# Hybrid SSD / RG-LRU layer on one core: the masked products of four chunks built and issued as one group

## The chip, the core and the metric

The program runs on one NeuronCore of a Trainium2 chip. The metric is the device time of one execution in microseconds (us); the kernel before was timed three times, with a median of 2409.85 us (2408.59 to 2413.37). One further execution was profiled; it took 2411.09 us.

## What is computed

One layer of a diffusion backbone over 1024 latent tokens of width 1024, with 256 context tokens as a prefix. A Mamba-2 SSD branch and an RG-LRU branch, both in two directions, are gated, merged and projected; a squared-ReLU MLP follows. Only the SSD branch matters here. Its core for one direction, cut down:

```
# 8 chunks of 128 tokens, 8 groups, 4 heads a group, head width 64, state 128
cum   = cumsum(dt * a_neg) within a chunk
seg   = cum[i] - cum[j];  decay = exp(where(i >= j, seg, -inf))
cb    = C @ B^T                                   # 128 x 128 per chunk and group
y     = (cb * decay) @ (x * dt)                   # the masked product, within a chunk
      + (C @ h_start) * exp(cum)                  # what the state before the chunk adds
h_start[k+1] = exp(cum_end) * h_start[k] + B^T @ (to_end * x * dt)
y_all = y_forward + flip(y_backward) + d * x
```

All arithmetic is fp32. Large products are made of three fp32r products of high and low parts; the small products of the SSD branch are plain fp32.

## The kernel before

The kernel is written tile by tile; a scheduler then puts the instructions of each engine in a fixed order by a priority (the place in the program text, moved by `tc.high_priority(offset=...)`) and by its own estimate of when operands are ready, and adds the semaphores. Each engine runs its own order strictly. Buffers come from pools: `bufs=n` says how many copies of a tile exist, and a copy is written again only when all readers of the last tile in it are done.

The part around the change is the SSD stage. It loops over 8 groups (`g`). For a group the projections of B, C and two 128-channel tiles of x are made (`proj`, `mm3`, lines 113 to 115, PSUM tiles `acc`), convolved and put through SiLU (lines 228 to 236, 441, 442). `cb` holds C times B for all 8 chunks. For each of the two tiles (`tl`, two heads each):

- the x tile is transposed to token order, `xt` (one buffer, named xtm in the trace);
- the states `H` of all chunk borders are built in both directions (line 519 on TensorE, 527 on VectorE; one buffer);
- two halves (`hf_`) of four chunks each follow. A half has three PSUM tiles `y[0]`, `y[1]`, `y[2]` (3 buffers for all). For each chunk `p`: ScalarE makes four 128x128 exponentials `L` (line 549) from `R`, which a DMA filled and GpSimd masked (line 544); VectorE adds the two directions into `M` (line 552) and multiplies by `cb` (553); TensorE forms the forward and the backward state product (555, 556) and, for each of the two heads, the masked product (558). The head's product has 64 output rows, so the two heads' products go to the two halves of `y[2]`'s partitions and use 64 columns of the array each;
- after the four chunks VectorE takes the three `y` tiles out of PSUM: lines 560 (twice), 562, 563, 564, 565; `u` goes to DRAM by a DMA and is squared on ScalarE (569).

Projections of the next tiles (`z_tile` and the next group's B, C, x) are issued by TensorE in between, as the scheduler finds place. A row sum `rp` (462) is put in when a group's squares are ready. Every fp32 matmul of the SSD stage is two records in the trace (two passes); an `acc` matmul is one.

Of the kernel before, what the change touches and what calls it, by code (L numbers as in the profile page):

```python
# [9 lines left out]
F32 = mybir.dt.float32  # L10
F32R = mybir.dt.float32r
AF = mybir.ActivationFunctionType
OP = mybir.AluOpType
# [42 lines left out]
def _ap(t, off, dims):  # L56
    return bass.AP(tensor=t.tensor, offset=t.offset + off, ap=dims)
# [3 lines left out]
def tile_hybrid_layer(ctx: ExitStack, tc: tile.TileContext, x, xc, wmod, win, wdt, lruw, wbs, wbl,  # L61
                      wout, w1, w2, vecs, rows, out, dbg=None, stop=None):
    nc = tc.nc
    V, A, P, G, Q = nc.vector, nc.scalar, nc.tensor, nc.gpsimd, nc.sync
# [53 lines left out]
    start = ctx.enter_context(ExitStack())  # L118
# [21 lines left out]
    for k in range(10):  # L140
        if k < KT:
            wm = sp_.tile([128, 2, 1024], F32, name="wm", bufs=4)
            Q.dma_start(wm, _ap(wmod, k * 128 * 1024, [[1024, 128], [8 * 128 * 1024, 2], [1, 1024]]))
            for j in range(4):
                P.matmul(mps[j], sc[:, k, :], wm[:, j // 2, (j % 2) * 512:(j % 2 + 1) * 512],
                         start=k == 0, stop=k == KT - 1)
# [320 lines left out]
    def z_tile(t):  # L467
        zts[t] = gp.tile([128, S], F32, name="z", bufs=2)

        def zcb(s, o, n, pt, zt=zts[t]):  # L470
            A.activation(zt[:, o:o + n], pt, AF.Tanh, scale=0.5)
            V.scalar_tensor_tensor(zt[:, o:o + n], zt[:, o:o + n], 1.0, pt, op0=OP.add, op1=OP.mult)
        proj(win[T_Z + t], (0, 1), zcb)


    dw2 = {m: dr.tile([128, 1024], F32, name=f"dw{m}") for m in (*range(4), *range(24, 28))}
    z_tile(0)
    for g in range(8):
        m_ = sorted(dw2)[g]
        Q.dma_start(dw2[m_], w2[m_])  # L480
        bf = gp.tile([128, TT], F32, name="bf", bufs=1)
        proj(win[T_B + g], (0, 1, 2), conv_silu(16 + g, bf))
        bt = gp.tile([128, 10, 128], F32, name="bt", bufs=1)
        to_token(bf, bt)
        xf = {}
        cf = gp.tile([128, S], F32, name="cf")
        proj(win[T_C + g], (0, 1), conv_silu(24 + g, cf))
        xf[0] = gp.tile([128, TT], F32, name="xf", bufs=3)
        proj(win[T_X + 2 * g], (0, 1, 2), conv_silu(2 * g, xf[0]))
        cb = gp.tile([128, 8, 128], F32, name="cb", bufs=1)  # L490
        for c0 in (0, 4):
            tp = misc((128, 4, 128))
            for c in range(c0, c0 + 4):
                P.matmul(tp[:, c - c0], bf[:, c * 128:(c + 1) * 128], cf[:, c * 128:(c + 1) * 128], start=True, stop=True)
            A.activation(cb[:, c0:c0 + 4], tp, AF.Copy)
        xf[1] = gp.tile([128, TT], F32, name="xf", bufs=3)
        proj(win[T_X + 2 * g + 1], (0, 1, 2), conv_silu(2 * g + 1, xf[1]))
        sqs = {}
        for tl in range(2):
            t = 2 * g + tl  # L500
            if tl == 1:
                z_tile(t)
            xt = gp.tile([128, 10, 128], F32, name="xtm", bufs=1)
            to_token(xf[tl], xt)

            H = gp.tile([128, 9, 2, 128], F32, name="H", bufs=1)
            for k0 in range(0, 9, 2):
                n = min(2, 9 - k0)
                xs = gp.tile([128, 2, 2, 128], F32, name="xs", bufs=2)
                for d_, KD in ((0, KF), (1, KB)):  # L510
                    c0 = min(KD[k0:k0 + n])
                    V.tensor_tensor(xs[:, d_, :n].rearrange("p c (h q) -> p c h q", h=2),  # L512
                                    xt[:, c0:c0 + n].rearrange("p c (h q) -> p c h q", h=2),
                                    wst[:, c0:c0 + n, d_ * 32 + 2 * t:d_ * 32 + 2 * t + 2, None].to_broadcast([128, n, 2, 64]),
                                    op=OP.mult)
                sp = misc((128, n, 2, 128))
                for k in range(k0, k0 + n):
                    for d_, KD in ((0, KF), (1, KB)):
                        P.matmul(sp[:, k - k0, d_], bt[:, KD[k]], xs[:, d_, KD[k] - min(KD[k0:k0 + n])], start=True, stop=True)  # L519
                for k in range(k0, k0 + n):  # L520
                    if k == 0:
                        A.activation(H[:, 0], sp[:, 0], AF.Copy)
                        continue
                    for d_ in range(2):
                        for h in range(2):
                            hs_2 = slice(h * 64, h * 64 + 64)
                            V.scalar_tensor_tensor(H[:, k, d_, hs_2], H[:, k - 1, d_, hs_2], dec[:, k, d_ * 32 + 2 * t + h:d_ * 32 + 2 * t + h + 1],  # L527
                                                   sp[:, k - k0, d_, hs_2], op0=OP.mult, op1=OP.add)
            for hf_ in range(2):
                y = [ps.tile([128, 512], F32, tag="y", bufs=3, name="y") for _ in range(3)]  # L530
                E = gp.tile([128, 2, 512], F32, name="E", bufs=1)
                for h in range(2):
                    Q.dma_start(E[h * 64:h * 64 + 64],
                                _ap(decum, t * 4096 + h * 1024 + hf_ * 512, [[0, 64], [2048, 2], [1, 512]]))
                for p in range(4):
                    c = hf_ * 4 + p
                    if p % 2 == 0:
                        R = gp.tile([128, 4, 256], F32, name="R", bufs=2)
                        Q.dma_start(R, _ap(dcum, t * 4096 + c * 128, [[0, 128], [1024, 4], [1, 256]]))

                        for d_ in range(2):
                            rv = R[:, 2 * d_:2 * d_ + 2, :].rearrange("p q (c i) -> p q c i", c=2)
                            sg = 1 if d_ == 0 else -1
                            G.affine_select(out=rv, in_=rv, compare_op=OP.is_ge, fill=-BIG, base=0,  # L544
                                            pattern=[[0, 2], [0, 2], [sg, 128]], channel_multiplier=-sg)
                    L = gp.tile([128, 4, 128], F32, name="L", bufs=2)
                    for q in range(4):
                        col = hf_ * 64 + (q // 2) * 32 + 2 * t + q % 2
                        A.activation(L[:, q], R[:, q, (p % 2) * 128:(p % 2 + 1) * 128], AF.Exp,  # L549
                                     bias=ncumT[:, p, col:col + 1])  # L550
                    M = gp.tile([128, 2, 128], F32, name="M", bufs=2)
                    V.tensor_tensor(M, L[:, 0:2], L[:, 2:4], op=OP.add)
                    V.tensor_tensor(M, M, cb[:, c, None, :].to_broadcast([128, 2, 128]), op=OP.mult)
                    sl = slice(p * 128, p * 128 + 128)
                    P.matmul(y[0][:, sl], H[:, 1 + c, 0], cf[:, c * 128:(c + 1) * 128], start=True, stop=True)
                    P.matmul(y[1][:, sl], H[:, 8 - c, 1], cf[:, c * 128:(c + 1) * 128], start=True, stop=True)  # L556
                    for h in range(2):
                        P.matmul(y[2][h * 64:h * 64 + 64, sl], xt[:, c, h * 64:h * 64 + 64], M[:, h], start=True, stop=True)  # L558
                for d_ in range(2):
                    V.tensor_tensor(E[:, d_], E[:, d_], y[d_], op=OP.mult)  # L560
                u = gp.tile([128, 512], F32, name="u", bufs=2)
                V.scalar_tensor_tensor(u, xf[tl][:, hf_ * 512:hf_ * 512 + 512], vec("dsk", t), y[2], op0=OP.mult, op1=OP.add)
                V.tensor_tensor(E[:, 0], E[:, 0], E[:, 1], op=OP.add)
                V.tensor_tensor(u, u, E[:, 0], op=OP.add)
                V.scalar_tensor_tensor(u, u, 0.5, zts[t][:, hf_ * 512:hf_ * 512 + 512], op0=OP.mult, op1=OP.mult)
                Q.dma_start(du[t][:, hf_ * 512:hf_ * 512 + 512], u)
                flush()
                sq = gp.tile([128, 512], F32, name="sq", tag=f"sq{tl}", bufs=2 - tl)
                A.activation(sq, u, AF.Square)
                sqs[tl, hf_] = sq  # L570
                if tl == 1:
                    V.tensor_tensor(sq, sq, sqs[0, hf_], op=OP.add)
                    pend.append((g, hf_, sq))
        if g < 7:
            z_tile(2 * g + 2)
            flush()
        else:
            for m in range(8, 16):
                merge_tile(m)
                flush()  # L580
        r8 = gp.tile([128, 8], F32, name="r8")
        Q.dma_start(r8, _ap(dss, g * 1024, [[8, 128], [1, 8]]))
        rsqrt_small(r8, r8, RMS_EPS, 8, scale=1.0 / 256.0)
        Q.dma_start(_ap(drs[g], 0, [[8, 128], [1, 8]]), r8)
# [399 lines left out]
    for th in range(2):  # L984
        tok = []
        for i in range(4):
            ti = th * 4 + i
            if ti < len(x0):
                xt = x0[ti]
# [275 lines left out]
```

## Time and profile before

| | |
|---|---|
| median of 3 runs | 2409.85 us |
| profiled execution | 2411.09 us, of it 2409.3 us span |
| TensorE busy, share of the span | 98 %, 11485 matmul records |
| VectorE, ScalarE, GpSimd busy | 76 %, 45 %, 10 % |
| granted TensorE clock, mean over the span | 0.991 |
| SSD stage | about 515 to 1324 us of the span |

TensorE has two rows in the profile: PE is the matmul, PEld the loading of the stationary operand, which lies beside earlier matmuls. A matmul's end is modelled, so "busy" says little about how densely TensorE works; the distance from one start to the next does.

### The profile page before, as it was taken

The page shows a single profiled execution, that of the slowest core. Times are in us where ns is not written, and L with a number is a line of the kernel's source. Part 1 is how long each engine was busy: PE and PEld are TensorE (multiplying, and loading weights), DVE is VectorE, ACT ScalarE, POOL GpSimd, SP SyncE. Part 2 cuts the span into 40 slices and gives each one's busy share as a digit, 9 for nine tenths or more (in the row PEclk, how much of TensorE's full clock was granted, in tenths as well). Part 3 has the DMA queues.
Part 4 walks back from the last instruction along what each step waited for, and adds up shares of the span by engine and source line. Part 5 has one row for each costly group of instructions (what it writes and reads, how often), then busy time and mean ns, then how long its engine had stood idle before and what let it go on. Part 6 is the DMA issues. An engine that isn't in the chain of part 4 may idle for free.

```text
span 2409.3 us, 31481 instructions
## 1 busy us (share of the span) xinstructions
PE 2351.3 (98%) x11485; PEld 1881.1 (78%) x11485; DVE 1841.8 (76%) x3240; ACT 1094.0 (45%) x1909; POOL 243.5 (10%) x253
## 2 busy tenths in 40 slices
PE   7998999999999999999999999999999999999998
PEld 3877888787888878787877887877778888788876
DVE  6986688778888887878888379676687554749998
ACT  2766765635343443444344354132266444435521
POOL 1000000001110110201010000000114332000004
PEclk9998999999999999999999999999999999999999
DMA  9422154323333342434333552277345333624132
GB/s 354 130 65 64 53 166 149 106 66 118 88 97 88 97 128 64 134 81 113 88 97 118 175 196 88 80 228 233 123 151 167 106 105 105 240 79 155 55 114 87
DMA packets 135235, 298.39 MB, mean 124 GB/s; under 512 B 14996, under 2 KB 47892, under 8 KB 134952
## 3 DMA queue, kind: packets, MB, share of 16 engines
q1 hardware_dynamic: 135080, 296.39, 38.7%
q8 instruction: 90, 1.47, 0.2%
q14 instruction: 65, 0.53, 0.1%
HBM read 245.40 MB, written 55.13 MB: 125 GB/s over the span
## 4 chain that ended last, share of the span: by engine, by line
PE 77%; DVE 11%; DMA 6%; ACT 3%; issue 2%; POOL 0%; SPq 0%; POOLq 0%; DVEq 0%; ACTq 0%
PE acc L114 11%; PE acc L115 11%; PE acc L113 11%; PE pd L115 4%; PE pd L113 4%; PE pd L114 4%; PE wp L114 3%; PE wp L115 3%; PE wp L113 3%; PE mo L114 3%; PE mo L115 3%; PE mo L113 3%; PE misc L519 2%; PE y L558 2%; PE y L556 1%
## 5 line engine op out<-in xcount | busy, mean ns | idle before, releaser
L114 PE MATMUL acc<-hl,wh 128*128 128x512 f32 (+1 forms) x1560 | 596.4, 382 | 0.6 <-DVE hl L182 0.6
L115 PE MATMUL acc<-hh,wl 128*128 128x512 f32 (+1 forms) x1560 | 594.2, 381 | 0.0
L113 PE MATMUL acc<-hh,wh 128*128 128x512 f32 (+1 forms) x1560 | 591.5, 379 | 2.6 <-ACT hh L177 2.6
L114 PEld LDWEIGHTS acc<-hl,wh 128*128 128x128 f32 x1560 | 295.5, 189 | 58.1 <-issue 12.9
L113 PEld LDWEIGHTS acc<-hh,wh 128*128 128x128 f32 x1560 | 295.4, 189 | 52.2 <-issue 3.1
L115 PEld LDWEIGHTS acc<-hh,wl 128*128 128x128 f32 x1560 | 295.4, 189 | 47.9 <-issue 4.5
L549 ACT ACTIVATE L<-R,cumT 128x128 f32<-128x128 f32 x512 | 163.5, 390 | 123.9 <-issue 58.1
L102 ACT ACTIVATE wh<-wr 128x1024 fp32r<-128x1024 f32 x113 | 119.5, 1057 | 212.5 <-PE acc L114 158.1
L544 POOL TENSOR_SCALAR_AFFINE_SELECT R<-R 128x512 f32<-128x512 f32 x128 | 95.1, 766 | 1112.2 <-DMA R<-dcum 687.3
L103 DVE TENSOR_TENSOR wl<-wr,wh 128x1024 fp32r<-128x1024 f32 x113 | 138.0, 1222 | 29.2 <-ACT wh L102 27.0
L114 PE MATMUL wp<-orl,olh 128*128 128x512 f32 x392 | 153.1, 391 | 2.1 <-DVE orl L611 2.1
L115 PE MATMUL wp<-orh,oll 128*128 128x512 f32 x392 | 152.6, 389 | 0.0
L113 PE MATMUL wp<-orh,olh 128*128 128x512 f32 x392 | 149.9, 390 | 0.3 <-DVE ba L659 0.3
L527 DVE SCALAR_TENSOR_TENSOR H<-H,dec,misc 128x64 f32<-128x64 f32 x512 | 104.9, 273 | 25.0 <-PE misc L519 24.1
L97 POOL TENSOR_TENSOR mv<-mv,mhalf 128x1 f32<-128x1 f32 x34 | 29.7, 874 | 789.2 <-DVE mv L96 778.7
L234 DVE SCALAR_TENSOR_TENSOR xf<-acc,cw,xf 128x504 f32<-128x504 f32 (+1 forms) x96 | 62.4, 650 | 37.3 <-ACT xf L228 35.6
L610 ACT ACTIVATE olh<-k 128x512 fp32r<-128x512 f32 x81 | 51.1, 631 | 86.1 <-PE wp L114 81.2
L114 PEld LDWEIGHTS wp<-orl,olh 128*128 128x128 f32 x392 | 73.6, 188 | 18.8 <-DVE orl L611 3.8
L113 PEld LDWEIGHTS wp<-orh,olh 128*128 128x128 f32 x392 | 74.0, 189 | 16.3 <-DVE ba L659 0.7
L950 DVE TENSOR_TENSOR xl<-wr,xh 128x512 fp32r<-128x512 f32 x75 | 67.3, 900 | 24.3 <-ACT xh L949 24.1
L115 PEld LDWEIGHTS wp<-orh,oll 128*128 128x128 f32 x392 | 73.6, 188 | 15.2
L519 PEld LDWEIGHTS misc<-xs,bt 128*128 128x128 f32 x576 | 77.1, 191 | 9.8 <-DVE xs L512 3.0
(347 smaller groups left out, 5027.5 us busy)
## 6 DMA issues: line engine op xcount, KB each, us to landing
wr<-in_win_dram SPq DMA_DIRECT2D x80, 512.0 KB, 3.7
R<-dcum SPq DMA_DIRECT2D x64, 512.0 KB, 5.2
wr<-in_w_dram SPq DMA_DIRECT2D x37, 512.0 KB, 4.2
wm<-in_wmod_dram SPq DMA_DIRECT2D x32, 512.0 KB, 3.6
E<-decum SPq DMA_DIRECT2D x64, 256.0 KB, 4.5
da<-r SPq DMA_DIRECT2D x64, 256.0 KB, 3.1
k<-da SPq DMA_DIRECT2D x26, 512.0 KB, 3.6
k<-in_w_dram SPq DMA_DIRECT2D x20, 512.0 KB, 4.2
```

What stands on the lines that cost most here:

```text
L102: A.activation(hi, src, AF.Copy)
L103: V.tensor_tensor(lo, src, hi.bitcast(F32), op=OP.subtract)
L113: P.matmul(pt, wh, mh, start=first, stop=False)
L114: P.matmul(pt, wh, ml, start=False, stop=False)
L115: P.matmul(pt, wl, mh, start=False, stop=last)
L234: V.scalar_tensor_tensor(dv[:, :, sh:], pv[:, :, :L - sh], w[k], dv[:, :, sh:], op0=OP.mult, op1=OP.add)
L519: P.matmul(sp[:, k - k0, d_], bt[:, KD[k]], xs[:, d_, KD[k] - min(KD[k0:k0 + n])], start=True, stop=True)
L527: V.scalar_tensor_tensor(H[:, k, d_, hs_2], H[:, k - 1, d_, hs_2], dec[:, k, d_ * 32 + 2 * t + h:d_ * 32 + 2 * t + h + 1], sp[:, k - k0, d ...
L544: G.affine_select(out=rv, in_=rv, compare_op=OP.is_ge, fill=-BIG, base=0, pattern=[[0, 2], [0, 2], [sg, 128]], channel_multiplier=-sg)
L549: A.activation(L[:, q], R[:, q, (p % 2) * 128:(p % 2 + 1) * 128], AF.Exp, bias=ncumT[:, p, col:col + 1])
L610: A.activation(hi, src, AF.Copy)
L950: V.tensor_tensor(ts[i][1], v, ts[i][0].bitcast(F32), op=OP.subtract)
```

## The change

A half's masks are made in one tile `M` of four chunks with one buffer (before: a tile for each chunk, two buffers). `L` holds two chunks in one buffer (before: one chunk, two buffers). VectorE adds the directions of two chunks in one instruction of 512 columns, twice in a half, and multiplies all four chunks by `cb` in one of 1024 columns. All y products of the half stand together after that: four forward state products, four backward ones, then the eight masked ones, and all of them at a priority 120 places later (`YLATE`). `u` has one buffer in place of two. The pool's size stays as it was: `M` grows by 2 KB a partition, `u` shrinks by 2 KB.

```diff
+    YLATE = -120
@@ the loop over halves
+                M = gp.tile([128, 4, 2, 128], F32, name="M", bufs=1)
                 for p in range(4):
...
-                    L = gp.tile([128, 4, 128], F32, name="L", bufs=2)
+                        L = gp.tile([128, 2, 4, 128], F32, name="L", bufs=1)
                     for q in range(4):
                         col = hf_ * 64 + (q // 2) * 32 + 2 * t + q % 2
-                        A.activation(L[:, q], R[:, q, (p % 2) * 128:(p % 2 + 1) * 128], AF.Exp,
+                        A.activation(L[:, p % 2, q], R[:, q, (p % 2) * 128:(p % 2 + 1) * 128], AF.Exp,
                                      bias=ncumT[:, p, col:col + 1])
-                    M = gp.tile([128, 2, 128], F32, name="M", bufs=2)
-                    V.tensor_tensor(M, L[:, 0:2], L[:, 2:4], op=OP.add)
-                    V.tensor_tensor(M, M, cb[:, c, None, :].to_broadcast([128, 2, 128]), op=OP.mult)
-                    sl = slice(p * 128, p * 128 + 128)
-                    P.matmul(y[0][:, sl], H[:, 1 + c, 0], cf[:, c * 128:(c + 1) * 128], start=True, stop=True)
-                    P.matmul(y[1][:, sl], H[:, 8 - c, 1], cf[:, c * 128:(c + 1) * 128], start=True, stop=True)
-                    for h in range(2):
-                        P.matmul(y[2][h * 64:h * 64 + 64, sl], xt[:, c, h * 64:h * 64 + 64], M[:, h], start=True, stop=True)
+                    if p % 2:
+                        V.tensor_tensor(M[:, p - 1:p + 1], L[:, :, 0:2], L[:, :, 2:4], op=OP.add)
+                V.tensor_tensor(M, M, cb[:, hf_ * 4:hf_ * 4 + 4, None, :].to_broadcast([128, 4, 2, 128]), op=OP.mult)
+
+                with tc.high_priority(offset=YLATE):
+                    for d_ in range(2):
+                        for p in range(4):
+                            c = hf_ * 4 + p
+                            P.matmul(y[d_][:, p * 128:p * 128 + 128], H[:, 8 - c if d_ else 1 + c, d_], cf[:, c * 128:(c + 1) * 128],
+                                     start=True, stop=True)
+                    for p in range(4):
+                        for h in range(2):
+                            P.matmul(y[2][h * 64:h * 64 + 64, p * 128:p * 128 + 128],
+                                     xt[:, hf_ * 4 + p, h * 64:h * 64 + 64], M[:, p, h], start=True, stop=True)
...
-                u = gp.tile([128, 512], F32, name="u", bufs=2)
+                u = gp.tile([128, 512], F32, name="u", bufs=1)
```

The order on TensorE before, in the second half of a group's second tile in the middle of the stage (`y<-M` is a masked product, `y<-cf,H` a state product, `acc` a projection, `rp` the row sum):

```order
3542 L113 MATMUL acc<-hh_280,wh 128x512
3543 L558 MATMUL y<-M,xtm 64x128 x2
3544 L114 MATMUL acc<-hl_281,wh 128x512
3545 L115 MATMUL acc<-hh_280,wl 128x512
3546 L462 MATMUL rp<-sq,ones 1x512
3547 L558 MATMUL y<-M,xtm 64x128 x2
3548 L113 MATMUL acc<-hh_282,wh 128x512
3549 L114 MATMUL acc<-hl_283,wh 128x512
3550 L558 MATMUL y<-M,xtm 64x128 x2
3551 L115 MATMUL acc<-hh_282,wl 128x512
```

The order on TensorE of the changed kernel, at the first half of such a tile; its lines are numbered up to eight higher, 565 is the masked and 561 the state product:

```order
3038 L114 MATMUL acc<-hl_279,wh 128x512
3039 L561 MATMUL y<-cf,H 128x128 x4
3040 L565 MATMUL y<-M,xtm 64x128 x8
3041 L561 MATMUL y<-cf,H 128x128 x8
3042 L115 MATMUL acc<-hh_278,wl 128x512
```

Masked products stood in 126 runs over the kernel, 124 of two and 2 of four matmuls; they now stand in 32 runs of eight. The state products' runs went from 151 to 72. The number of matmuls is the same.

The order on VectorE before, between the end of a first half and the second half's masks, in a group's first tile:

```order
768 L563 TENSOR_TENSOR E<-E 128x512
769 L562 SCALAR_TENSOR_TENSOR u<-xf,vt,y 128x512
770 L552 TENSOR_TENSOR M<-L 128x256
771 L564 TENSOR_TENSOR u<-u,E 128x512
772 L553 TENSOR_TENSOR M<-M,cb 128x256
773 L565 SCALAR_TENSOR_TENSOR u<-u,z 128x512
774 L552 TENSOR_TENSOR M<-L 128x256 x2
775 L553 TENSOR_TENSOR M<-M,cb 128x256 x2
```

The same place on VectorE in the changed kernel (554 is the addition, 555 the product with `cb`):

```order
724 L568 TENSOR_TENSOR E<-E,y 128x512
725 L571 TENSOR_TENSOR E<-E 128x512
726 L570 SCALAR_TENSOR_TENSOR u<-xf,vt,y 128x512
727 L554 TENSOR_TENSOR M<-L 128x512
728 L572 TENSOR_TENSOR u<-u,E 128x512
729 L573 SCALAR_TENSOR_TENSOR u<-u,z 128x512
730 L554 TENSOR_TENSOR M<-L 128x512
731 L555 TENSOR_TENSOR M<-M,cb 128x1024
```

The masks of the second half are now two additions and one product, all behind the first half's `u`, which reads `y[2]`. ScalarE has five exponentials, a square, and three exponentials between the two additions. On TensorE eight state products and 23 projections stand between the two halves' masked groups there. After the SSD stage, from the last merge tiles on, all engines' orders are the same as before.

## Rows read from the trace of the kernel before

**Rows 1.** The page, part 1: busy us, share of the span, instructions.

```profile
PE 2351.3 (98%) x11485; PEld 1881.1 (78%) x11485; DVE 1841.8 (76%) x3240; ACT 1094.0 (45%) x1909; POOL 243.5 (10%) x253
```

**Rows 2.** Busy times of the SSD stage; PEclk is the granted clock's share.

```profile
core 0: us, PE busy (x) PEld busy (x) DVE busy (x) ACT busy (x) POOL busy (x), PEclk, DMA share, GB/s
515.00:1324.00 809.00, 806.60 (x4617) 643.42 (x4616) 671.93 (x1576) 349.22 (x804) 101.18 (x127) 1.00 0.36 101
```

**Rows 3.** All waits of TensorE's matmuls in it: us in total, times, longest.

```profile
PE y L555 <- DVE H L527: 0.9, 2, 0.5
```

**Rows 4.** Timeline of TensorE matmuls near the stage's end: start, length, line, tiles, count.

```profile
1319.18 0.39 PE L114 MATMUL acc<-hl,wh 128*128 128x512 f32 x1
1319.50 0.44 PE L558 MATMUL y<-M,xtm 128*64 128x128 f32 x4
1319.87 0.50 PE L115 MATMUL acc<-hh,wl 128*128 128x512 f32 x1
1320.21 0.39 PE L113 MATMUL acc<-hh,wh 128*128 128x512 f32 x1
1320.44 0.39 PE L114 MATMUL acc<-hl,wh 128*128 128x512 f32 x1
...
1323.21 0.66 PE L558 MATMUL y<-M,xtm 128*64 128x128 f32 x8
1323.80 0.50 PE L113 MATMUL acc<-hh,wh 128*128 128x512 f32 x1
```

**Rows 5.** The same view where masked products stand between state products.

```profile
993.28 0.49 PE L556 MATMUL y<-cf,H 128*128 128x128 f32 x2
993.70 0.44 PE L558 MATMUL y<-M,xtm 128*64 128x128 f32 x4
994.07 0.71 PE L556 MATMUL y<-cf,H 128*128 128x128 f32 x4
994.62 0.83 PE L555 MATMUL y<-cf,H 128*128 128x128 f32 x6
```

**Rows 6.** Timeline of the weight loads at Rows 4's places; idle before, releaser.

```profile
1319.50 0.20 PEld L558 LDWEIGHTS y<-M,xtm 128*64 128x64 f32 x4 [0.36 <-issue]
1319.87 0.19 PEld L115 LDWEIGHTS acc<-hh,wl 128*128 128x128 f32 x1 [0.17 <-issue]
...
1323.21 0.42 PEld L558 LDWEIGHTS y<-M,xtm 128*64 128x64 f32 x8 [0.86 <-DVE M L553]
```

**Rows 7.** Waits of weight loads in the stage: us in total, times, longest.

```profile
PEld y L558 <- issue: 13.1, 39, 0.4
PEld y L558 <- DVE M L553: 3.8, 9, 0.9
```

**Rows 8.** VectorE's groups of the stage by form: busy us, mean ns, idle before.

```profile
L103 DVE TENSOR_TENSOR wl<-wr,wh 128x1024 fp32r<-128x1024 f32 x45 | 54.8, 1217 | 3.2 <-ACT wh L102 3.2
L553 DVE TENSOR_TENSOR M<-M,cb 128x256 f32<-128x256 f32 x126 | 54.2, 437 | 0.6
L552 DVE TENSOR_TENSOR M<-L 128x256 f32<-128x256 f32 x126 | 54.2, 434 | 33.8 <-PE y L558 22.2 <-ACT L L549 8.7 <-issue 1.8
L560 DVE TENSOR_TENSOR E<-E,y 128x512 f32<-128x512 f32 x62 | 41.0, 681 | 3.1 <-PE y L556 1.6 <-DMA E<-decum 1.5
L562 DVE SCALAR_TENSOR_TENSOR u<-xf,vt,y 128x512 f32<-128x512 f32 x32 | 23.9, 745 | 12.2 <-PE y L558 12.2
L564 DVE TENSOR_TENSOR u<-u,E 128x512 f32<-128x512 f32 x31 | 21.6, 696 | 0.0
```

**Rows 9.** Timeline of ScalarE: a square and a chunk's four exponentials.

```profile
1000.23 0.63 ACT L569 ACTIVATE sq<-u 128x512 f32<-128x512 f32 x1 [0.21 <-DVE u L565]
1000.77 1.26 ACT L549 ACTIVATE L<-R,cumT 128x128 f32<-128x128 f32 x4
```

**Rows 10.** Timeline, all engines: an addition and the exponentials that reuse its `L`.

```profile
998.24 0.42 DVE L552 TENSOR_TENSOR M<-L 128x256 f32<-128x256 f32 x1
...
998.74 1.28 ACT L549 ACTIVATE L<-R,cumT 128x128 f32<-128x128 f32 x4 [2.21 <-issue]
```

## The prediction

> **What bounds the kernel now.** I read the page's first part, then the windows, the waits of TensorE, and the timelines around the masked products. The page shows TensorE busy for 98 % of the span and nobody else above 76 % [rows 1]. In the SSD stage it is 806.60 of 809.00 us at a granted clock of 1.00, that is 2.4 GHz, with VectorE at 83 % and ScalarE at 43 % [rows 2], and its matmuls waited for another engine for 0.9 us in all [rows 3]. So the stage lasts as long as TensorE's list of instructions lasts, and a change in it is worth what it takes out of that list. The list is not dense, and the busy share hides it: the reader is to look at starts. A projection starts 0.23 us after the one before (1320.21 to 1320.44). With four records of masked products in between, the way from one projection's start (1319.18) to the start of the second one behind the block (1320.21) is 1.03 us, 0.57 more than two steps of 0.23 [rows 4]. Four records themselves occupy 0.37 of it (1319.50 to 1319.87); the rest is a late start ahead of the block (0.32 for 0.23) and a slow first projection behind it (0.34 for 0.23). Between state products it is the same: a record there takes 0.11; the two ahead of the block at 993.70 need 0.42 and the four behind it 0.55, so each first record behind a block is 0.11 late and the last one ahead 0.09, and 0.37 + 0.11 + 0.09 is again 0.57 [rows 5]. The weight loads tell why: the engine loads no weights for 0.36 us ahead of each block and 0.17 behind it, with "issue" as the reason [rows 6]; 39 of the blocks' gaps of that kind sum to 13.1 us [rows 7].
>
> One block at the stage's end holds eight records, since two chunks' products met there. From its start to the next projection are 0.59 us, 0.22 more than with four [rows 4], and its weights load for 0.42 against 0.20 [rows 6]. So four further records in a running block cost 0.22, and a block of their own costs 0.57: each block that is merged into another is worth 0.35 us.
>
> The Trainium skill ("TensorEngine Tiling (Array Packing)", Tiling Modes) says that changing the tiling mode, not just the tile, drains TensorE. The two gaps agree: they stand only where 128x64 weights follow 128x128 ones or the reverse. The page gives no price, so the sum goes by the rows.
>
> **The change part by part.**
>
> *Masked products in groups.* In the two orders 124 blocks of four records and 2 of eight become 32 of sixteen. Before: 124 x 0.57 + 2 x 0.79 = 72.3 us. After, a block of sixteen: 0.57 + 3 x 0.22 = 1.23, times 32 = 39.4. TensorE's list shortens by 32.9 us. No block of sixteen stands in the trace; the bounds for a further four records are 0.22 (the block of eight, whose weights load without a pause) and 0.37 (all of a block of four from its start to the next instruction). By the upper one the group costs 0.57 + 3 x 0.37 = 1.68, and the gain falls to 18.5. Below 0.22 nothing is to be expected, since 0.42 for eight loads is already twice 0.20. I take 0.22, the nearer row.
>
> *State products in groups.* Same records at 0.11; their runs fall from 151 to 72. They use the array as the projections do and no gap like that of the masked ones stands ahead of them, so I price this at nothing; the bounds are zero and one record's 0.11 for each of 79 runs, a gain of up to 8.7.
>
> *VectorE.* Per half, before: four additions of 0.434 and four products of 0.437 are 3.48 us. After: two additions of 512 columns at 0.70 (as line 564) and one product of 1024 at 1.22 (as line 103) are 2.62 [rows 8]. That is 0.86 a half and 28 us over 32 halves, on an engine that is idle for 137 us of the stage. It lies beside TensorE and is worth nothing by itself.
>
> *The new wait.* Before, a chunk's product needs its own mask alone. After, the sixteen records wait for all four masks, and with one `M`, nothing may be written into it until the last half's group is done. In the first half of a tile this costs nothing: its masks can be made during the projections of the tile and stand on VectorE ahead of the states. The second half's have to fit between the two groups. Worked out in a group's first tile, from the first half's first masked record: VectorE takes the product and the sum on `E` (0.68 and about 0.7), which waited for the state products only, and is at `u` after about 1.5 us; `u` 0.75; addition 0.70; five exponentials at 1.26/4 = 0.32, the square 0.63 that stands among them, three more: 3.2 [rows 9], since the one `L` is free only when the first addition has read it (the handover took 998.74 - 998.66 = 0.08 in before) [rows 10]; addition 0.70; product 1.22. Together 1.5 + 0.75 + 0.70 + 0.1 + 3.2 + 0.70 + 1.22 = 8.2, and 0.2 for the handover to TensorE, 8.4 us. TensorE has in the meantime: the rest of the first group, 1.0; sixteen state records at 0.11 and the slow first one, 1.9; 23 projections at 0.23 with a slow first and the late start, 5.5: 8.4 us. It is a draw. In a group's second tile, three more projections and a row sum stand there, and on VectorE two steps of the convolution and a weight split more; I take it as a draw too. Queued behind the waiting masked product on TensorE are all projections, and so everything. A draw means that some of the 16 second halves are late by a few tenths: I take 0.2 us each, 3.2 us. The bounds are 0 and, if the cover counted for nothing, 16 x 8.4 = 134 us; the nearest row is that of masks in before, where 9 gaps of weight loads that ended with a mask sum to 3.8 us, 0.36 of each being the switch, so 0.6 us of real lateness in all [rows 7]. That row lies near zero, so I stay near zero.
>
> The Trainium skill ("Perfetto Trace Analysis", Optimizing Scalar/DVE Operations) speaks against this part: where VectorE and ScalarE aren't saturated but cause bubbles on other engines, breaking instructions up may let work complete sooner. The change does the reverse, on engines at 83 and 43 %. In the trace of before they cause almost none (the 0.6 us above), so the rule would bite only if the draw is lost; its time is that of the second rival below.
>
> *Other buffers.* One `u`: its DMA and its square have until the next half's `u`, over 6 us later by the same chain; nothing. The lower priority moves no weight load and no DMA on SP's queue past another that TensorE waits for within the stage; behind the stage the orders are the same.
>
> **The sum.** 2411.1 (the profiled execution) - 32.9 + 3.2 = 2381.4 us. The profiled execution is 1.2 above the median of the runs, so 2380.
>
> **The rivals.**
>
> 1. *The wait eats everything and more (slower).* The chain of the second half's masks takes longer than its cover by over 32.9 / 16 = 2.06 us on average, for instance because ScalarE or VectorE stands, in its fixed order, at a convolution that waits for TensorE. With 2.5 us: 2411.1 - 32.9 + 40 = 2418, by the median 2417. For it: the draw, and that exponentials already waited for an addition and VectorE for TensorE (22.2 us at line 552 [rows 8]). Against it: those waits were of engines with time to spare. It decides from a chain of about 10.5 us. Chance 0.04.
> 2. *The wait eats part.* About 1 us at each of the 16: 2411.1 - 32.9 + 16 = 2394, by the median 2393. Chance 0.14.
> 3. *The long group doesn't keep the pace*, 0.37 for each further four: 2411.1 - 18.5 + 3.2 = 2396, by the median 2395. Against it: the loads of the block of eight. Chance 0.05.
> 4. *TensorE's list isn't the bound after all*, the gaps are filled by something else that was late anyway: no change, 2410. Against it: 0.9 us of waits. That the groups are not formed is excluded by the order. Chance 0.03.
> 5. *The forecast*, 2371 to 2390: 0.74.
>
> **How the numbers follow.** The low end takes no new wait and a part of the state products' bound: 2409.9 - 32.9 - 6 = 2371. To the other side the forecast reaches to 2390; the second and third rival carry the range to 2396, which leaves out the upper half of these two, the first, the fourth, and a little at the low end. A measurement of this kernel tells 0.2 %, about 5 us, from no change. Faster by more than that: forecast, second and third rival, 0.93; same 0.03; slower 0.04.
>
> **What would show it.** In the profile after: blocks of sixteen masked records of about 1.0 us from their start to the next instruction; the gap of 0.36 in the weight loads 32 times and not 126; VectorE busy about 28 us less; the SSD stage some 30 us shorter and all else as long as before. Wrong I would be if TensorE waits for the product with `cb` ahead of second halves' groups for more than a few tenths, or if records inside the group stand further apart than two in 0.11 us.

## The result, and the profile after

The changed kernel takes 2382.35 us (median of 4 runs, 2381.16 to 2383.17) where the kernel before takes 2411.61 us (4 runs beside it, 2408.59 to 2414.23): a ratio of 0.9873, 95 % interval 0.9861 to 0.9885. In a later set it was 2376.78 us against 2408.72, ratio 0.9864 (0.9850 to 0.9878). The profiled execution took 2381.16 us. The page's first part:

```profile
PE 2320.9 (98%) x11485; PEld 1885.0 (79%) x11485; DVE 1826.4 (77%) x3080; ACT 1091.1 (46%) x1909; POOL 249.9 (11%) x253
```

The busy times of the SSD stage (columns as in [rows 2]):

```profile
515.00:1294.00 779.00, 775.17 (x4616) 647.22 (x4616) 654.04 (x1419) 342.39 (x791) 105.41 (x125) 1.00 0.35 103
```

TensorE's 4616 records of the stage, 4617 in [rows 2], now take 779 us, not 809, at the same granted clock of 1.00. Busy shares have not moved: 98 % against 98 % [rows 1].

The end of the stage is best fixed by TensorE's own list, which is the same set of matmuls from the first transpose of the first group's B to the first matmul of the next stage (`wp`). In the kernel before that way is 953.30 us (465.00 to 1418.30). The start and the end of it after, in the timeline of TensorE (start, length, line, tiles):

```profile
465.29 0.60 PE L450 MATMUL misc<-ident,bf 128*128 128x128 f32 x4
...
1389.34 0.39 PE L113 MATMUL wp<-orh,olh 128*128 128x512 f32 x1
```

That is 924.05 us, 29.3 less, and the medians of the runs differ by 29.26. So the whole gain lies in this stretch. Below it is called the stretch; in a second profiled execution of the changed kernel it was 923.12 us. What lies behind it varies more between executions of one kernel: 990.0 us in the first and 986.0 in the second.

A masked group now, on TensorE (timeline, second half of a group's second tile), answers to [rows 4]:

```profile
1197.11 0.40 PE L113 MATMUL acc<-hh,wh 128*128 128x512 f32 x1
1197.44 1.09 PE L565 MATMUL y<-M,xtm 128*64 128x128 f32 x16
1198.46 0.50 PE L114 MATMUL acc<-hl,wh 128*128 128x512 f32 x1
1198.80 0.39 PE L115 MATMUL acc<-hh,wl 128*128 128x512 f32 x1
```

From 1197.11 to 1198.80 are 1.69 us; two steps of 0.23 taken off, the group costs 1.23 us, the value of the forecast's sum. The timeline of the weight loads at the same place answers to [rows 6]:

```profile
1197.44 0.85 PEld L565 LDWEIGHTS y<-M,xtm 128*64 128x64 f32 x16 [0.36 <-issue]
1198.46 0.19 PEld L114 LDWEIGHTS acc<-hl,wh 128*128 128x128 f32 x1 [0.17 <-issue]
```

Their waits in the stage answer to [rows 7] (us in total, times, longest):

```profile
PEld misc L450 <- DVE xtm L452: 8.2, 18, 1.0
PEld y L565 <- issue: 5.7, 16, 0.4
PEld rp L462 <- DVE sq L580: 3.0, 6, 0.8
```

The gaps are as long as before and stand once around sixteen records: 0.17 behind each group, 0.36 ahead of the 16 groups that follow a projection, and 0.12 ahead of the other 16, which follow state products. Before it was the same: 0.12 ahead of the 63 runs behind state products, 0.35 or 0.36 ahead of 47 of the 55 behind projections (0.25 at the other eight), and 0.86 ahead of the eight behind row sums. So [rows 6], on which the forecast rests "0.36 us ahead of each block", are the places behind projections. No masked group's loads wait for a mask: the row of `y` at 565 has "issue" alone. The row of before for the transposes, against the 8.2 above:

```profile
PEld misc L450 <- DVE xtm L452: 2.0, 7, 0.3
```

TensorE's matmul waits have grown from the one row of [rows 3] to three:

```profile
PE misc L450 <- DVE xtm L452: 1.6, 4, 0.5
PE misc L520 <- DVE xs L513: 1.3, 6, 0.3
PE rp L462 <- DVE sq L580: 0.7, 3, 0.3
```

They are on transposes, states and row sums, not on the masks.

The chain of the forecast's "draw", in a group's first tile (timeline of PE, DVE and ACT, in order of time; the brackets give the idle time before and what ended it):

```profile
1048.23 1.09 PE L565 MATMUL y<-M,xtm 128*64 128x128 f32 x16
1048.33 0.69 DVE L568 TENSOR_TENSOR E<-E,y 128x512 f32<-128x512 f32 x1 [2.30 <-PE y L561]
...
1049.66 0.74 DVE L570 SCALAR_TENSOR_TENSOR u<-xf,vt,y 128x512 f32<-128x512 f32 x1
1050.32 0.69 DVE L554 TENSOR_TENSOR M<-L 128x512 f32<-128x512 f32 x1
1051.09 1.57 ACT L551 ACTIVATE L<-R,cumT 128x128 f32<-128x128 f32 x5 [9.35 <-issue]
...
1053.09 0.97 ACT L551 ACTIVATE L<-R,cumT 128x128 f32<-128x128 f32 x3
1054.10 0.69 DVE L554 TENSOR_TENSOR M<-L 128x512 f32<-128x512 f32 x1 [1.76 <-ACT L L551]
1054.82 1.23 DVE L555 TENSOR_TENSOR M<-M,cb 128x1024 f32<-128x1024 f32 x1
1056.16 0.39 PE L115 MATMUL acc<-hh,wl 128*128 128x512 f32 x1
1056.47 1.09 PE L565 MATMUL y<-M,xtm 128*64 128x128 f32 x16
```

The order is the one that the forecast walked through. The masks are done 7.82 us after the first group's start (1054.82 + 1.23 = 1056.05), where 8.2 was worked out; the second group starts 0.31 behind the projection ahead of it, which is the late start of a switch of shape (0.32 in [rows 4]) and nothing more. In the eight first tiles the masks end 0.41 to 0.43 us ahead of the second group, in the second tiles 1.08 to 1.09 (in the last one 0.62), and no group of the 32 starts over 0.10 later behind its predecessor than an even step.

The first halves' groups start with the same lateness, though their masks are done 13 to 34 us ahead. VectorE's last instruction for the masks of the group at 1048.23:

```profile
1015.19 1.26 DVE L555 TENSOR_TENSOR M<-M,cb 128x1024 f32<-128x1024 f32 x1
```

The state products ahead of that group on TensorE:

```profile
1047.24 1.06 PE L561 MATMUL y<-cf,H 128*128 128x128 f32 x8
```

The masks are done at 1016.45, the eight records ahead take 8 x 0.111 = 0.89 us, and the group starts 0.99 behind the first of them, 0.1 late. A late mask can't be the reason there.

### The profile page after: what moved, and what is told of

Same layout as the page of the kernel before. It is cut to its first block, busy times and chain, and to the rows that moved or that the text cites. A ratio compares the mean times of both kernels' runs of the same rounds, so it can differ in the third digit from the quotient of the medians.

```text
span 2379.3 us, 31288 instructions
## 1 busy us (share of the span) xinstructions
PE 2320.9 (98%) x11485; PEld 1885.0 (79%) x11485; DVE 1826.4 (77%) x3080; ACT 1091.1 (46%) x1909; POOL 249.9 (11%) x253
## 4 chain that ended last, share of the span: by engine, by line
PE 72%; DVE 15%; DMA 7%; ACT 3%; issue 2%; POOL 0%; SPq 0%; POOLq 0%; DVEq 0%; ACTq 0%
PE acc L113 11%; PE acc L114 11%; PE acc L115 11%; PE pd L115 4%; PE pd L113 4%; PE pd L114 4%; PE misc L520 3%; PE mo L114 2%; PE mo L113 2%; PE mo L115 2%; PE wp L114 2%; PE wp L115 2%; PE wp L113 2%; PE y L561 2%; PE op L1006 1%
## 5 line engine op out<-in xcount | busy, mean ns | idle before, releaser
L115 PE MATMUL acc<-hh,wl 128*128 128x512 f32 (+1 forms) x1560 | 588.2, 377 | 0.0
L546 POOL TENSOR_SCALAR_AFFINE_SELECT R<-R 128x512 f32<-128x512 f32 x128 | 100.2, 808 | 1077.5 <-DMA R<-dcum 1007.9
L103 DVE TENSOR_TENSOR wl<-wr,wh 128x1024 fp32r<-128x1024 f32 x113 | 138.8, 1229 | 28.4 <-ACT wh L102 26.3
```

The costliest lines, as they stand in the source:

```text
L103: V.tensor_tensor(lo, src, hi.bitcast(F32), op=OP.subtract)
L115: P.matmul(pt, wl, mh, start=False, stop=last)
```

## Experiments

Four theories stood at the start. A: each run of masked products costs TensorE a switch of array shape, 0.35 us beyond its records, and 94 runs fewer are the gain. B: the fewer and wider instructions of VectorE are. C: the later priority of the state products is. D: the gaps before were late masks, not a switch. The first halves' groups above already speak against D. The result alone can't tell A from B and C, as the change does all three.

**Wide masks, products apart.** The changed kernel with the products written per chunk again:

```diff
-                with tc.high_priority(offset=YLATE):
-                    for d_ in range(2):
-                        for p in range(4):
+                for p in range(4):
...
+                    with tc.high_priority(offset=YLATE):
+                        for d_ in range(2):
...
-                    for p in range(4):
+                    with tc.high_priority(offset=YLATE - 15 * p):
```

> Masks as in the change (one M of four chunks, wide additions and product on VectorE), but the masked products get priorities 15 places apart, so that they stand in 87 runs and not 32. Theory A (each run of 128x64 products costs TensorE 0.35 us for going into that shape and out of it): 55 more runs, +19 us over the changed kernel, 2401, 0.996 of before. Theory B (the gain is VectorE's 28 us less work in fewer, wider instructions): nothing lost, 2382, 0.988. Theory C (the gain is the later priority of the state products): nothing lost, 2382.

Measured 2406.31 us (10 runs, 2399.80 to 2409.99) beside 2410.04 of before: ratio 0.9982 (0.9973 to 0.9992). Nearly all the gain is gone though the masks are as wide as in the change and VectorE is busy for no longer (1823.7 us by the page, 1826.4 in the change); B and C, as they were put, have no room for that. A's direction held, its number didn't: 2401 was expected. The timeline of TensorE shows why:

```profile
994.25 0.38 PE L562 MATMUL y<-cf,H 128*128 128x128 f32 x2
994.57 0.43 PE L566 MATMUL y<-M,xtm 128*64 128x128 f32 x2
994.93 0.49 PE L562 MATMUL y<-cf,H 128*128 128x128 f32 x2
```

Here many runs hold one head's matmul alone (x2). From its start to the next instruction are 0.36 us (994.57 to 994.93), as long as for four records, both heads', in [rows 4] (0.37). So a run of one head costs 0.56 and not the 0.46 that a half of the records had suggested. With 46 runs of one matmul, 9 of two, 16 of four and 16 of eight the list gives 46 x 0.56 + 9 x 0.57 + 16 x 0.79 + 16 x 1.23 = 63.2 us against 39.4: 23.8 over the change, 2406.2. That was worked out after the run; the 64 runs below were made to test it. In the profiled execution the stretch is 952.0 us, 27.9 over the change's; of the 4 left over, waits of weight loads for the transposes' copies (9.7 us against 8.2) and for the row sums' squares (5.4 against 3.0) are 3.9.

**Narrow masks, products grouped.** The reverse: VectorE's instructions narrow as before, TensorE's order the change's.

```diff
-                        L = gp.tile([128, 2, 4, 128], F32, name="L", bufs=1)
+                    L = gp.tile([128, 4, 128], F32, name="L", bufs=2)
...
+                    V.tensor_tensor(M[:, p], L[:, 0:2], L[:, 2:4], op=OP.add)
+                for j in range(0, 128, 32):
+                    V.tensor_tensor(M[:, :, :, j:j + 32], M[:, :, :, j:j + 32],
+                                    cb[:, hf_ * 4:hf_ * 4 + 4, None, j:j + 32].to_broadcast([128, 4, 2, 32]), op=OP.mult)
```

> Products grouped as in the change (32 runs of eight), but VectorE does the masks in additions of 256 columns, one a chunk, and four products of 256 columns a half, as many and as wide as before, with L one chunk and two buffers as before. Theory A: the gain stays but for new waits of a few us, 2382 to 2388. Theory B: the gain goes with VectorE's 28 us, about 2410.

Measured 2380.87 us, ratio 0.9876 (0.9862 to 0.9891); the stretch is 923.11 us. All of the gain without the wide instructions: B falls.

**No late priority.** `YLATE = 0` in place of -120; the masked products still stand in 32 runs of sixteen records, the state products in 96 runs (before 151, after 72).

> The changed kernel with YLATE 0: still 32 runs of eight masked products, state products less grouped. Theory A: 2382 within 5 us. Theory C: the gain is lost in good part, 2395 to 2410.

Measured 2383.32 us, ratio 0.9886 (0.9871 to 0.9900). The gain stays: C falls. The stretch is 928.0 us, 3.9 more than the change's, so the priority may be worth a few us; the medians, 1 us apart and of two sets, don't settle it.

**The kernel before, masked products at full width.** Here the shape is taken away and the order kept: x in token order is padded with zeros, so that each head's product has 128 output rows and both heads add up in one PSUM tile.

```diff
+    xz = gp.tile([128, 8, 256], F32, name="xz", bufs=1)
...
-                        P.matmul(y[2][h * 64:h * 64 + 64, sl], xt[:, c, h * 64:h * 64 + 64], M[:, h], start=True, stop=True)
+                        P.matmul(y[2][:, sl], xz[:, c, h * 128:h * 128 + 128], M[:, h], start=h == 0, stop=h == 1)
```

> The kernel before, with the masked products at full width: each head's x stands in 128 columns of which the other head's 64 are zero, and the two heads' products are added up in PSUM. Chunk by chunk as before, 128 runs of two, but no 128x64 weights are left; the array does twice the work, four records of 0.11 us after each other where two pairs ran side by side. Theory A: 512 x 0.11 = 57 us in place of 72, 16 us faster than before, 2396, 0.9935. Rival D (the gaps ahead of masked products are late masks, whatever the shape of the weights): the gaps stay and the doubled work comes on top, 28 us slower, 2440, 1.012.

Measured 2433.39 us, ratio 1.0101 (1.0084 to 1.0118): near D's number. As a time it decides nothing, since the edit disturbed more than the shape. The timeline of TensorE at one of the products:

```profile
1010.14 0.40 PE L114 MATMUL acc<-hl,wh 128*128 128x512 f32 x1
1010.37 0.61 PE L568 MATMUL y<-M,xz 128*128 128x128 f32 x4
1010.74 0.48 PE L115 MATMUL acc<-hh,wl 128*128 128x512 f32 x1
```

The weight loads there:

```profile
1009.91 0.19 PEld L114 LDWEIGHTS acc<-hl,wh 128*128 128x128 f32 x1
1010.22 0.57 PEld L568 LDWEIGHTS y<-M,xz 128*128 128x128 f32 x4
```

TensorE's longest wait in the stage:

```profile
PE misc L512 <- DVE xz L514: 19.1, 8, 2.7
```

At the products A's reading holds: the late start and the gap of 0.36 are gone. The product starts 0.23 behind the projection (0.32 in [rows 4]) and its loads 0.12 behind the end of the ones ahead, though it still needs its mask, and D would have kept it late. What made the kernel slower is a new wait: 19.1 us, eight times, for the padded copy, which in this order stands on VectorE behind masks whose inputs come late. The masked products themselves became cheaper, though their records do twice the work. Add up over all their runs, in the trace, the distances from start to start up to the next instruction, the lateness of the first record and that of the second instruction behind: 72.3 us in the kernel before (the forecast's sum) and 63.0 here. A had said 57 and D 28 more than before, so A has the direction and a part of the size, and D fails.

**Masks in 64 runs.** The dose between: the changed kernel, with the products again written chunk by chunk and a priority that falls by 6 a chunk.

```diff
-                    for p in range(4):
+                    with tc.high_priority(offset=YLATE - 6 * p):
```

> The changed kernel, but the masked products of a chunk are again written after that chunk's state products, with a priority that falls by 6 a chunk: wide masks and all else stay. In the order on TensorE the second halves come out as one run of eight matmuls each (16 runs); of the first halves the first chunk's two matmuls stand apart, one by one (32 runs of one), and the other six as one run (16 runs of six): 64 runs in place of 32, the same 256 matmuls. Theory A (each run has a price, .35 us and .22 for every four records, and a run of one matmul costs .56): 16 x 1.23 + 16 x 1.01 + 32 x .56 = 53.8 us against 39.4, so +14.4 over the change: 2396.7 us, ratio 0.994. Theory B or C (the wide masks or the later state products made the change faster): as the change, 2382, ratio 0.988.

Measured 2394.53 us (5 runs, 2392.62 to 2396.36), ratio 0.9935 (0.9923 to 0.9948), where A said 2396.7 and 0.994. Against the change in the same set (2376.78) the medians differ by 17.8 us. The stretch is 937.93 us, 14.8 over the second execution of the change, of that set; A's sum said 14.4. A first half in the timeline:

```profile
1055.10 0.43 PE L566 MATMUL y<-M,xtm 128*64 128x128 f32 x2
1055.46 0.49 PE L562 MATMUL y<-cf,H 128*128 128x128 f32 x2
1055.88 0.43 PE L566 MATMUL y<-M,xtm 128*64 128x128 f32 x2
...
1056.88 0.88 PE L566 MATMUL y<-M,xtm 128*64 128x128 f32 x12
```

Three runs where the change has one. With 126, 87, 64 and 32 runs A's sums lie 32.9, 23.8, 14.4 and 0 us over the change's; the ratios 1, 0.9982, 0.9935 and 0.9873, taken of 2410 us, lie 30.6, 26.3, 14.9 and 0 over it (17.1 for the 64 runs, against the 0.9864 of their own set). The times alone tell 87 runs from 126 badly: the stretch of 952.0 us is only 1.3 under that of before, since 7.9 of the 9.2 us by which the runs became cheaper came back elsewhere. The runs' own cost tells them apart. Counted in the traces as for the full-width kernel it is 72.3, 63.1, 53.6 and 39.2 us, where A's sums are 72.3, 63.2, 53.8 and 39.4.

**The row sum at full width, twice.** The row sum's weights are one column wide (128*1), also a shape apart. Here they are 128:

```diff
-                rp = misc((1, 512), "rp")
-                P.matmul(rp, ones[:, 0:1], sq, start=True, stop=True)
+                rp = misc((128, 512), "rp")
+                P.matmul(rp, ones, sq, start=True, stop=True)
```

> The changed kernel, and the 16 row sums of squares use all 128 columns of ones as weights in place of one column; the product takes as long, one row of the result is used. Theory A, if a one-column weight is such a shape too: three late starts of 0.09, 0.09 and 0.11 around each go, 16 x 0.3 = 4.7 us, 2377.6, 0.998 of the changed kernel (0.9854 of before). Theories B and C: no change, 2382.

Measured 2375.65 us (4 runs, 2373.95 to 2381.95), ratio 0.9854 (0.9837 to 0.9870): as expected to the fourth digit, and 6.7 us under the change's median, which is of another set. So both were run again side by side:

> The changed kernel itself, beside the next one on the same chip: 2382 us, ratio 0.988.

> The changed kernel with the row sum's weights 128 columns wide in place of one, as run before (2375.65 us, ratio 0.9854), now beside the change on the same chip. If a row sum's one-column weights cost TensorE a switch of shape, each of the 16 gets some .3 to .45 us cheaper: 5 to 7 us under the change, 2375 to 2377. If the earlier difference was one between chips, the two agree within 2 us.

Measured 2376.78 us (0.9864, 0.9850 to 0.9878) for the change and 2376.60 us (0.9859, 0.9843 to 0.9875) for the full-width row sum: no difference that these runs can tell. What looked like agreement at first is not borne out beside the change; two sets of the change itself differ by 5.6 us. The timeline of TensorE in the change at a row sum:

```profile
1194.58 0.39 PE L113 MATMUL acc<-hh,wh 128*128 128x512 f32 x1
1194.90 1.02 PE L462 MATMUL rp<-sq,ones 128*1 128x512 f32 x2
1195.85 0.50 PE L114 MATMUL acc<-hl,wh 128*128 128x512 f32 x1
1196.19 0.39 PE L115 MATMUL acc<-hh,wl 128*128 128x512 f32 x1
```

The same row sum at full width:

```profile
1193.41 0.39 PE L113 MATMUL acc<-hh,wh 128*128 128x512 f32 x1
1193.64 1.02 PE L462 MATMUL rp<-sq,ones 128*128 128x512 f32 x2
1194.10 0.79 PE L114 MATMUL acc<-hl,wh 128*128 128x512 f32 x1
1194.73 0.39 PE L115 MATMUL acc<-hh,wl 128*128 128x512 f32 x1
```

The wait of its weight loads there:

```profile
PEld rp L462 <- DVE sq L580: 4.5, 7, 1.0
```

The switch is there: 1.61 us from the projection ahead to the second one behind, against 1.32 without it, so 0.29 here and 4.6 us if it held at all sixteen. But the stretch shrank by 0.5 us only (923.12 to 922.60). Over the sixteen places the steps around row sums fell by 2.4 us and not by 4.6, in part since they now wait for the squares (weight loads 4.5 us, in the change's execution beside 3.2), and the steps ahead of transposes grew by about 1. That is what the forecast's fourth rival describes, in small: a gap closed ahead of something that was late anyway.

## Why the prediction was right

It said 2380 us, 29.7 less than the kernel before; the median is 2382.35, and 2376.78 in the second set, 29.3 and 31.9 less than before in the same sets. That the first agrees to half a microsecond is in part luck: the 3.2 us taken off for a wait of the masks were lost, but not at the masks.

- *The price of a run and the groups' sum* (-32.9): right. A group costs the 1.23 us that was carried over from one block of eight. Take every distance between neighbouring starts in the stretch and subtract an even step (0.227 for a projection, 0.111 for a state record, 0.055 for a masked one): what is left at masked products and their neighbours fell from 43.5 to 11.0 us, -32.5 (some tenths of this count hang on which neighbour a step is given to; the count of the experiments has -33.1). The bound with 0.37 for each further four didn't come; in the group two records start every 0.109 us. That the price belongs to a run is shown by the doses, that the switch of shape is its cause by the late start and the gap of 0.36, which went with the shape in the full-width kernel. That is as the Trainium skill has it ("TensorEngine Tiling (Array Packing)", Tiling Modes): changing the mode drains TensorE; the price, 0.35 us a run, is from the rows here.
  Two readings behind the term were loose, without harm to the sum, which goes by starts. The gap of 0.36 in the loads was to come 32 times in place of 126: it comes 16 times, and came 55 times (eight of them 0.25), since behind state products it is 0.12. And the 0.6 us of "real lateness" of masks in [rows 7] was none: eight of the nine gaps are the usual 0.36, and the ninth, 0.86, stands behind a row sum, where all eight gaps are 0.86 whatever ended them.
- *State products in groups* (0): nothing to be seen of the grouping; 96 runs of them in place of 72 made 2383.32 against 2380.87 in the same set, with intervals that overlap. But the first state products of a half were late in the kernel before, where weight loads waited for the states `H` (5.0 us, eight times), and no longer are: 3.1 us in the count of steps below, 2.8 with 96 runs. The forecast had no term for that.
- *VectorE* (28 us less, worth nothing): worth nothing is right, by the narrow masks. The 28 was mis-sized: the page has 15.4 us less. The instructions' lengths in [rows 8] overlap on VectorE; what counts is the step from start to start. In the kernel before:

```profile
999.18 0.42 DVE L553 TENSOR_TENSOR M<-M,cb 128x256 f32<-128x256 f32 x1
999.51 0.69 DVE L565 SCALAR_TENSOR_TENSOR u<-u,z 128x512 f32<-128x512 f32 x1
1000.11 0.78 DVE L552 TENSOR_TENSOR M<-L 128x256 f32<-128x256 f32 x2
```

In the changed kernel:

```profile
1192.40 1.22 DVE L103 TENSOR_TENSOR wl<-wr,wh 128x1024 fp32r<-128x1024 f32 x1
1193.54 0.69 DVE L580 TENSOR_TENSOR sq<-sq 128x512 f32<-128x512 f32 x1
```

  The steps are 0.33 for 256 columns, 0.60 for 512, 1.14 for 1024. A half goes from 8 x 0.33 = 2.64 to 2 x 0.60 + 1.14 = 2.34, 0.30 less, some 10 us over 32 halves; what the other 5 are was not followed. Little of it hangs on the widths: in the run with narrow masks, with 3240 instructions as before, the page has 1831.3 us, 10.5 of the 15.4 less as well.
  The Trainium skill ("Perfetto Trace Analysis", Optimizing Scalar/DVE Operations) was weighed against the wide instructions: breaking them up may let work complete sooner where they cause bubbles on other engines. With the masks narrow the ratio is 0.9876, with them wide 0.9873; no run here shows the rule at work, since no group waits for its masks in either.
- *The new wait* (+3.2 at second halves' masks): the size came true by luck, at another place. The draw was met to 0.4 us, and all sixteen groups start with the switch's lateness alone, so this term measured 0. But the stretch fell by 29.3 and not by 32.5: 3.2 us came back at work that the forecast did not price. By the same count of steps, those ahead of transposes grew by 3.7 us, those at states by 0.9, and those around row sums by 2.3 (eight of them stood next to a masked run before and shared its switch); the lateness of the first state products shrank by 3.1 and the projections among themselves by 1.1; the rest is below 1 us each. The transposes' weight loads wait for the copies of earlier ones out of PSUM, 8.2 us in the rows above, 2.0 in the row of before. One such place behind the second group of a first tile, in the timeline of VectorE and the weight loads:

```profile
1057.62 0.75 DVE L570 SCALAR_TENSOR_TENSOR u<-xf,vt,y 128x512 f32<-128x512 f32 x1 [1.57 <-PE y L565]
1059.20 1.29 DVE L568 TENSOR_TENSOR E<-E,y 128x512 f32<-128x512 f32 x2 [0.84 <-DMA E<-decum]
1060.41 0.68 DVE L452 COPY xtm<-misc 128x512 f32<-128x512 f32 x1
1061.14 0.42 PEld L450 LDWEIGHTS misc<-ident,xf 128*128 128x128 f32 x4 [0.83 <-DVE xtm L452]
```

  `u` waits for the group on VectorE, then `E` for its DMA, and the copy that frees the transposes' PSUM tile stands behind both. VectorE's waits for that DMA are 7.2 us in the stage (1.5 at the same line in [rows 8]). That this is the cause of the transposes' 3.7 us was read from the timeline and not tested by an edit. The forecast asked what is queued behind the waiting product on TensorE, but not what is queued on VectorE behind the readers of a product that is moved later.
- *The rest of the sum*: the stages behind are as long as before within what executions of one kernel differ by.

The rivals. The wait did not eat the gain (first and second): no group waited. The long group kept its pace (third). TensorE is the bound (fourth), but not without a remainder: of what its list lost, a tenth came back, and of the row sums' 4.6 us nearly all.

## What to carry to other kernels

Where TensorE looks full, lay the starts of its matmuls side by side: a gap that returned at each change of the weights' shape was a price per run here, and grouping runs of one shape took it out without a change to the arithmetic. Price it from two run lengths in the trace, and then ask of each engine's fixed order what the later group delays, above all copies that free PSUM for the same engine. Judge a few us by a stretch between two fixed matmuls, or by runs side by side: two sets of one kernel lay 5.6 us apart here.

## What the runs showed of the hardware that was not expected

- A run with one head's matmul takes as long as a run with both: 0.36 against 0.37 us from its start to the next instruction. Inside a group the two heads' records start 6 to 7 ns apart and then 102 ns pass, two in 0.109 us, as in one step of a full-width record (0.11).
- Weights of one column are a shape of their own: with 128 columns the same row sum starts 0.23 and not 0.32 behind the projection, and the second projection behind it starts 1.09 and not 1.29 us after it. So the forecast's sentence that the gaps stand only where 128x64 weights meet 128x128 ones leaves these out.
